# A hybrid SSM, attention and convolution layer on Trainium2: one modulation moved from TensorE to VectorE rows, another shared with GpSimd

## The chip, the cores and the metric

The kernel runs on one core of a Trainium2 chip. The metric is the device time of one execution in microseconds (us), the median over several. A core has TensorE (PE in the profile, with its weight loads as PEld), VectorE (DVE), ScalarE (ACT), GpSimd (POOL) and SyncE (SP), which here issues nearly all DMA transfers. Each engine takes its instructions in a fixed order and waits on semaphores for the others.

## What is computed

One layer of a decoder, 256 tokens, width 2048, float32. It has a token mixer and a gated MLP, each behind an RMSNorm whose scale and shift, and whose gate on the way out, come from a conditioning vector:

```python
cond = jax.nn.silu(c)
mod = cond @ w_mod[l] + b_mod[l]
sh1, sc1, gt1, sh2, sc2, gt2 = jnp.split(mod, 6, axis=-1)
h = rms_norm(x, g_pre_mix[l]) * (1.0 + sc1[:, None]) + sh1[:, None]
y = hybrid_mixer(h, ...)
x = x + gt1[:, None] * rms_norm(y, g_post_mix[l])
h = rms_norm(x, g_pre_ffn[l]) * (1.0 + sc2[:, None]) + sh2[:, None]
y = conv_ffn(h, w_up[l], ffn_conv_w[l], w_down[l])
x = x + gt2[:, None] * rms_norm(y, g_post_ffn[l])
```

The mixer projects `h` to an SSM branch, an attention branch, a convolution branch and three gates of width 2048; `merged` is the sum of the gated branches, and `merged @ w_o` its output. The change concerns `mod`: a vector times a matrix of 2048 x 12288, of which `sc1, sh1` are called half 0, `sc2, sh2` half 1, and `gt1`, `gt2` the two gate modulations.

## The kernel before

**Weights.** All large products are made in fp32r from two parts: a weight tile of 128x1024 is loaded into one of four `raw` buffers, ACT rounds it to `hi` (L72), DVE subtracts to get `lo` (L73, called a split below), and PE makes three products (`mm3`, L123 to L125). `hi` and `lo` have four buffers each; `next_weights` keeps two tiles ahead of the one in use (AHEAD). A stage is therefore a chain of such tiles: four groups of the in-projection (80 tiles), the convolution branch with the attention beside it (24), gate 0, gate 1 and gate 2 (40 each: f = 0 to 15, with two tiles of the gate's projection each and one of the branch's output per two f), the first output projection (32), then the MLP.

**Fillers.** Work that does not belong to the main chain is written as generators that a `Filler` advances at a rate per tick, two ticks per f: the attention, the SSM (beside gates 0 and 1; tables `T`, pairs `M1`, `M2`), the modulations. The language's scheduler then orders each engine's instructions by readiness and priority, so an instruction may stand earlier than it was written.

**Modulation.** Half 1 (`mods2`) has eight groups g of 256 channels. Groups 0 to 3 go by rows on DVE: eight tiles a group, each loaded by `raw_tile` and multiplied with the conditioning row and summed along the row in one instruction (L191), so 32 rows. Groups 4 to 7 (PE_MOD) go on PE (`mod_rows_pe`, `modps`, L152): per four tiles of the sum four matmuls with a 32 column weight, then ACT copies the sums and PE transposes them (`mfps`, L175). Their tiles come alternately through `raw` and one buffer `mraw`. The first gate modulation (`mod_gate`, `gg`) is filled into gate 2 and the output projection: for two halves b of 1024 channels, 16 tiles each (`dx`, five buffers, three loads ahead), DVE accumulates `acc` (L216), then PE sums over the partitions with a matrix of ones (`ggps`, L224).

Of the kernel before, what the change touches and what calls it, by code (L numbers as in the profile page):

```python
# [8 lines left out]
F32 = mybir.dt.float32  # L9
# [6 lines left out]
P = 128  # L16
# [12 lines left out]
LAG = False  # L29
PE_MOD = ((), (4, 5, 6, 7))  # L30

# [18 lines left out]
def kernel(  # L50
# [62 lines left out]

    def next_weights():
        while len(queue) < 1 + AHEAD:
            src = next(stream, None)
            if src is None:
                break
            queue.append(weights(*src))
        return queue.pop(0)  # L120

# [43 lines left out]
    def mod_half(half, g, A_scale, A_shift, vg, vsc, vsh, lag=True):  # L165
        mf = cp.tile([P, 4], F32, tag="mf", name="mf", bufs=2)
        if g in PE_MOD[half]:
            i = PE_MOD[half].index(g)
            res = []
            yield from mod_rows_pe(lambda j: wmod_h[half][i, j], res)  # L170
            if lag:
                yield
            ps = psB.tile([P, 512], F32, tag="B", name="mfps")
            for i in range(4):
                nc.tensor.transpose(  # L175
                    ps[:, P * i : P * i + P], res[0][:, P * i : P * i + P], marks["ident"]
                )
            nc.vector.tensor_reduce(
                mf, ps.rearrange("p (i q r) -> p i q r", i=4, q=4)[:, :, :, 0], AX.X, ALU.add
            )  # L180
        else:
            i = [n for n in range(8) if n not in PE_MOD[half]].index(g)
            mp2 = cp.tile([P, 4, 2], F32, tag="mp2", name="mp2", bufs=2)
            for q in range(4):
                for kc in range(2):
                    if half == 0:
                        w = mp.tile([P, 1024], F32, tag="bo", name="mraw", bufs=6)
                        nc.sync.dma_start(w, wmod_t[half][i, 2 * q + kc])
                    else:
                        w = raw_tile(wmod_t[half][i, 2 * q + kc])  # L190
                    nc.vector.scalar_tensor_tensor(  # L191
                        w, w, 1.0, cond_row[kc], ALU.mult, ALU.mult, accum_out=mp2[:, q, kc : kc + 1]
                    )
                    if q * kc < 3:
                        yield
            nc.vector.tensor_reduce(mf, mp2, AX.X, ALU.add)
# [10 lines left out]

    def mod_gate(which, gg, load, depth):
        for b in range(2):
            acc = sp.tile([P, 1024], F32, tag="acc", name="acc")  # L210
            nc.sync.dma_start(acc, brow[which, b])
            ws = [load(wmod_g[which, b, kt]) for kt in range(depth)]
            for kt in range(KT):
                if kt + depth < KT:
                    ws.append(load(wmod_g[which, b, kt + depth]))
                nc.vector.scalar_tensor_tensor(  # L216
                    acc, ws.pop(0), cond[:, kt : kt + 1], acc, ALU.mult, ALU.add
                )
                yield
            yield  # L220
            for i in range(2):
                c = slice(512 * i, 512 * i + 512)
                ps = psB.tile([P, 512], F32, tag="B", name="ggps")
                nc.tensor.matmul(ps, ones, acc[:, c], start=True, stop=True)  # L224
                nc.vector.tensor_mul(gg[b][:, c], ps, gg[b][:, c])
# [42 lines left out]
    def out_proj(nj, act, gg, ss, yg, tail, filler=None, held=4):  # L268
        for n in range(4):
# [10 lines left out]
            for j in range(cut):  # L280
# [3 lines left out]
                for t in range(2):  # L284
                    mms(j, w, t)
            last = [next_weights() for _ in range(nj - cut)]
            if n == 2:
                dummy = cp.tile([P, 1], F32, tag="dummy", name="dummy")
                nc.scalar.activation(dummy, ss[:, 0, 0:1], AF.Sqrt)
            for t in range(2):  # L290
                for j in range(cut, nj):
                    mms(j, last[j - cut], t)
                with ExitStack() as es:
# [7 lines left out]
                    if n == 3:  # L301
                        tail(t)

    with ExitStack() as mx:
# [330 lines left out]
        def glu(zp):  # L635
# [3 lines left out]
            for f in range(4):  # L639
                ps = psB.tile([P, 512], F32, tag="B", name="glups")  # L640
                for kt in range(4):
                    w = wg[kt // 2]
                    c = 512 * (kt % 2) + P * f
                    mm3(
                        ps[:, :S], w[0][:, c : c + P], w[1][:, c : c + P], gqh[:, kt], gql[:, kt],
                        kt == 0, kt == 3,
# [8 lines left out]
        def ssm_all(zp):  # L655
# [3 lines left out]
            yield  # L659
            gqh = mp.tile([P, 4, S], F32R, tag="bo", name="gqh", bufs=6)  # L660
            gql = mp.tile([P, 4, S], F32R, tag="bo", name="gql", bufs=6)
            ssm_st["g"] = (gq, gqh, gql)
            M1s = [mp.tile([P, 2, S], F32, tag="uv", name="M1", bufs=20) for _ in range(8)]
            M2s = [mp.tile([P, 2, S], F32, tag="uv", name="M2", bufs=20) for _ in range(8)]
            Ts = {}
# [25 lines left out]
            for j in range(4):  # L691
                mm = []
                for q in range(4):
# [12 lines left out]
                    ts_ = T[:, 1].unsqueeze(1).to_broadcast([P, 2, S])  # L706
                    M1, M2 = M1s[s % 8], M2s[s % 8]
                    mm.append((M1, M2))
# [26 lines left out]
                nc.scalar.activation(gq[:, j], yv, AF.Gelu_apprx_tanh)  # L735
                split(gq[:, j], gqh[:, j], gql[:, j])
            glu(zp)
# [47 lines left out]
        fa = fill(attention_all())  # L785
        run(conv_branch(), (fa, 3.5), (m2, 2))
        fa.finish()
# [3 lines left out]
        fs = fill(ssm_all(zp))  # L791
        run(gate_branch(0, 2), (fs, 0.7), (m2, 2))
        run(gate_branch(1, 1), (fs, 0.75), (m2, 1.5))
        fs.finish()
        m2.finish()
        zs.close()
# [10 lines left out]

        mg = fill(mod_gate(0, gg, load_late, 3))
        run(gate_branch(2, 0), (mg, 1.5))
        mg.rate = 1.0  # L810
# [216 lines left out]
```

## Time and profile before

| | us |
|---|---|
| runs, median (lowest, highest) | 1648.1 (1645.53, 1648.68) |
| profiled execution, its own time | 1650.52 |
| its span, first to last instruction | 1648.7 |
| PE busy | 1581.9 |
| DVE busy | 1217.1 |
| ACT busy | 810.2 |
| POOL busy | 61.8 |
| convolution and attention | 284 to 391 |
| gate 0, gate 1, gate 2 | 391 to 536, to 681, to 790 |
| first output projection | 790 to 881 |

The profile shows one execution. Busy time is the union of an engine's instructions; PE's matmuls are pipelined, so the durations of single matmuls overlap. A window gives the busy time of each engine in a stretch of the span; a wait is put down to what released the engine.

### The profile page before, as it was taken

The numbers are of one execution on the slowest core, as the hardware profiler recorded it, in microseconds if no ns is written. First come the engines' busy times: TensorE is split into PE (matmuls) and PEld (weight loads), VectorE is DVE, ScalarE is ACT, GpSimd is POOL, SyncE is SP. The second block draws the span as 40 slices with busy tenths as digits, with TensorE's granted clock in tenths as the row PEclk, the third lists the DMA queues.
The fourth block names the chain that finished last, engine by engine and source line by source line (L and its number), as shares of the span: only waits on it lengthen the run. The fifth ranks groups of instructions, "written<-read, shape, count | busy, mean of one in ns | idle before, by whom it ended". The sixth has DMA issues, their size and how long they took to land.

```text
span 1648.7 us, 26062 instructions
## 1 busy us (share of the span) xinstructions
PE 1581.9 (96%) x10104; PEld 1398.0 (85%) x10104; DVE 1217.1 (74%) x1854; ACT 810.2 (49%) x1219; POOL 61.8 (4%) x102
## 2 busy tenths in 40 slices
PE   2999899999999999999998999999999999999997
PEld 1989889889888899999887888888888888888886
DVE  5889986896787798787757788778888767444444
ACT  2554333655445454544446555555555555344342
POOL 0000940000000000000000000000000000000000
PEclk7999999999999999999999999999999999999999
DMA  8988876777776665888864777767777665666553
GB/s 315 371 322 295 308 263 195 232 248 244 257 258 249 223 225 164 300 315 323 286 190 141 231 240 230 231 217 230 240 233 230 203 192 182 190 190 189 187 188 126
DMA packets 107404, 389.56 MB, mean 236 GB/s; under 512 B 11920, under 2 KB 12048, under 8 KB 107280
## 3 DMA queue, kind: packets, MB, share of 16 engines
q1 hardware_dynamic: 105552, 382.00, 69.1%
q10 hardware_dynamic: 1728, 5.90, 1.0%
q8 instruction: 79, 1.29, 0.3%
q14 instruction: 45, 0.37, 0.1%
HBM read 385.75 MB, written 2.10 MB: 235 GB/s over the span
## 4 chain that ended last, share of the span: by engine, by line
PE 79%; DVE 9%; DMA 6%; ACT 3%; issue 2%; POOL 0%; SPq 0%; DVEq 0%; ACTq 0%
PE ups L876 20%; PE ups L877 10%; PE ops L125 7%; PE ops L124 7%; PE ops L123 7%; PE gps L123 5%; PE gps L125 5%; PE gps L124 5%; PE inps L125 3%; PE inps L124 3%; PE inps L123 3%; DVE lo L73 3%; DMA raw<-in_wmod_t 3%; DMA raw<-in_wB 1%; DVE mraw L191 1%
## 5 line engine op out<-in xcount | busy, mean ns | idle before, releaser
L73 DVE TENSOR_TENSOR lo<-raw,hi 128x1024 fp32r<-128x1024 f32 x520 | 636.1, 1228 | 283.6 <-ACT hi L72 281.8
L72 ACT CAST hi<-raw 128x1024 fp32r<-128x1024 f32 x520 | 541.8, 1047 | 570.1 <-PE ops L125 173.8
L876 PE MATMUL ups<-h2p,hi 128*128 128x512 f32 x1408 | 495.3, 394 | 0.1
L877 PE MATMUL ups<-h2p,lo 128*128 128x256 f32 x1408 | 398.1, 283 | 0.0
L876 PEld LDWEIGHTS ups<-h2p,hi 128*128 128x128 f32 x1408 | 264.4, 188 | 61.7 <-ACT hi L72 0.5
L877 PEld LDWEIGHTS ups<-h2p,lo 128*128 128x128 f32 x1408 | 264.7, 188 | 0.6 <-issue 0.5
L123 PE MATMUL gps<-hh,hi 128*128 128x256 f32 x768 | 219.3, 286 | 0.0
L125 PE MATMUL gps<-hh,lo 128*128 128x256 f32 x768 | 216.5, 282 | 2.1 <-DVE lo L73 2.1
L124 PE MATMUL gps<-hl,hi 128*128 128x256 f32 x768 | 216.4, 282 | 0.0
L123 PEld LDWEIGHTS gps<-hh,hi 128*128 128x128 f32 x768 | 144.9, 189 | 15.3 <-issue 8.0
L123 PE MATMUL inps<-hh,hi 128*128 128x256 f32 x448 | 128.2, 287 | 23.6 <-ACT hi L72 23.6
L125 PEld LDWEIGHTS gps<-hh,lo 128*128 128x128 f32 x768 | 144.7, 188 | 2.3 <-DVE lo L73 2.3
L124 PEld LDWEIGHTS gps<-hl,hi 128*128 128x128 f32 x768 | 144.8, 189 | 0.2 <-issue 0.2
L123 PE MATMUL ops<-hi,ah 128*128 128x512 f32 x352 | 138.9, 395 | 0.0
L124 PE MATMUL ops<-lo,ah 128*128 128x512 f32 x352 | 138.9, 395 | 0.0
L125 PE MATMUL ops<-hi,al 128*128 128x512 f32 x352 | 138.9, 395 | 0.0
L125 PE MATMUL inps<-hh,lo 128*128 128x256 f32 x448 | 128.3, 289 | 4.4 <-DVE lo L73 4.4
L124 PE MATMUL inps<-hl,hi 128*128 128x256 f32 x448 | 127.6, 286 | 0.0
L123 PEld LDWEIGHTS inps<-hh,hi 128*128 128x128 f32 x448 | 86.4, 193 | 24.4 <-ACT hi L72 24.2
L125 PEld LDWEIGHTS inps<-hh,lo 128*128 128x128 f32 x448 | 85.8, 192 | 6.0 <-DVE lo L73 6.0
L191 DVE SCALAR_TENSOR_TENSOR mraw<-mraw,cond_row 128x1024 f32<-128x1024 f32 x64 | 78.4, 1236 | 16.1 <-DMA mraw<-in_wmod_t 16.1
L124 PEld LDWEIGHTS inps<-hl,hi 128*128 128x128 f32 x448 | 86.2, 193 | 0.1
(244 smaller groups left out, 2324.1 us busy)
## 6 DMA issues: line engine op xcount, KB each, us to landing
raw<-in_wup SPq DMA_DIRECT2D x176, 512.0 KB, 4.2
raw<-in_wB SPq DMA_DIRECT2D x120, 512.0 KB, 4.5
raw<-in_wdn SPq DMA_DIRECT2D x88, 512.0 KB, 3.6
raw<-in_wA SPq DMA_DIRECT2D x80, 512.0 KB, 5.1
mraw<-in_wmod_t SPq DMA_DIRECT2D x64, 512.0 KB, 5.5
raw<-in_wmod_t SPq DMA_DIRECT2D x32, 512.0 KB, 4.5
dx<-in_wmod_g SPq DMA_DIRECT2D x32, 512.0 KB, 6.5
raw<-in_wo SPq DMA_DIRECT2D x32, 512.0 KB, 4.0
```

The lines of the kernel that those rows point to most:

```text
L72: marks["act"] = nc.scalar.copy(hi, src)
L73: nc.vector.tensor_sub(lo, src, hi)
L123: nc.tensor.matmul(dst, wh, ah, start=first, stop=False)
L124: nc.tensor.matmul(dst, wh, al, start=False, stop=False)
L125: nc.tensor.matmul(dst, wl, ah, start=False, stop=last)
L191: nc.vector.scalar_tensor_tensor(w, w, 1.0, cond_row[kc], ALU.mult, ALU.mult, accum_out=mp2[:, q, kc : kc + 1])
L876: nc.tensor.matmul(ps, wh[:, c], hp, start=kt == 0, stop=False)
L877: nc.tensor.matmul(ps[:, 0], wl[:, c], hp[:, 0], start=False, stop=kt == KT - 1)
```

## The change

All eight groups of half 1 go as DVE rows (PE_MOD is empty for both halves), 64 rows instead of 32. Their tiles no longer use `raw_tile` but one buffer `mraw`, whose load is issued one step ahead of its row. The filler's rates are 1.4, 1.2, 1.2 and 1.4 instead of 2, 2 and 1.5, and it now runs on into gate 2. In the first gate modulation every tile with an odd number goes to GpSimd, which scales it by the condition and adds it to two tiles `accp` of 512 columns; a second matmul per half of 512 columns adds `accp` to `ggps`. The SSM gets six pairs M1 and M2 instead of eight, and `gqh`, `gql` lie in other buffers. `out_proj` looks ahead less at the end of its last tiles and fetches one tile after each half of the tokens instead.

```diff
-PE_MOD = ((), (4, 5, 6, 7))
+PE_MOD = ((), ())
...
-    def next_weights():
-        while len(queue) < 1 + AHEAD:
+    def prefetch(n):
+        while len(queue) < n:
...
+    def next_weights(ahead=AHEAD):
+        prefetch(1 + ahead)
         return queue.pop(0)
...
+            def load(n):
+                tag, bufs = ("bo", 6) if half == 0 else ("mraw", 1)
+                w = mp.tile([P, 1024], F32, tag=tag, name="mraw", bufs=bufs)
+                nc.sync.dma_start(w, wmod_t[half][i, n])
+                return w
+
             for q in range(4):
                 for kc in range(2):
-                    if half == 0:
-                        w = mp.tile([P, 1024], F32, tag="bo", name="mraw", bufs=6)
-                        nc.sync.dma_start(w, wmod_t[half][i, 2 * q + kc])
-                    else:
-                        w = raw_tile(wmod_t[half][i, 2 * q + kc])
+                    w = load(2 * q + kc)
+                    if half == 1:
+                        yield
                     nc.vector.scalar_tensor_tensor(
                         w, w, 1.0, cond_row[kc], ALU.mult, ALU.mult, accum_out=mp2[:, q, kc : kc + 1]
                     )
...
-    def mod_gate(which, gg, load, depth):
+    def mod_gate(which, gg, load, depth, split_with=None):
...
+                w = ws.pop(0)
+                if split_with is not None and kt % 2:
+                    for i in range(2):
+                        c = slice(512 * i, 512 * i + 512)
+                        k = cond[:, kt : kt + 1]
+                        if kt == 1:
+                            part.append(split_with())
+                            nc.gpsimd.tensor_scalar(part[i], w[:, c], k, None, ALU.mult)
+                        else:
+                            nc.gpsimd.tensor_scalar(w[:, c], w[:, c], k, None, ALU.mult)
+                            nc.gpsimd.tensor_add(part[i], part[i], w[:, c])
+                else:
+                    nc.vector.scalar_tensor_tensor(
+                        acc, w, cond[:, kt : kt + 1], acc, ALU.mult, ALU.add
+                    )
                 yield
...
-                nc.tensor.matmul(ps, ones, acc[:, c], start=True, stop=True)
+                nc.tensor.matmul(ps, ones, acc[:, c], start=True, stop=not part)
+                if part:
+                    nc.tensor.matmul(ps, ones, part[i], start=False, stop=True)
...
-            last = [next_weights() for _ in range(nj - cut)]
+            last = [next_weights(min(AHEAD, nj - 1 - j)) for j in range(cut, nj)]
...
+                prefetch(t + 1)
...
-            M1s = [mp.tile([P, 2, S], F32, tag="uv", name="M1", bufs=20) for _ in range(8)]
+            M1s = [mp.tile([P, 2, S], F32, tag="uv", name="M1", bufs=20) for _ in range(6)]
...
-        run(conv_branch(), (fa, 3.5), (m2, 2))
+        run(conv_branch(), (fa, 3.5), (m2, 1.4))
...
-        run(gate_branch(0, 2), (fs, 0.7), (m2, 2))
-        run(gate_branch(1, 1), (fs, 0.75), (m2, 1.5))
+        run(gate_branch(0, 2), (fs, 0.7), (m2, 1.2))
+        run(gate_branch(1, 1), (fs, 0.75), (m2, 1.2))
...
-        run(gate_branch(2, 0), (mg, 1.5))
+        run(gate_branch(2, 0), (mg, 1.5), (m2, 1.4))
+        m2.finish()
```

The order of the instructions shows the change at three places. The first is SP's queue of transfers at the start of gate 0 (`raw<-in_wB`, `in_wbr`: weight tiles; `in_wmod_t`: tiles of the half-1 rows; `in_wmod_h`: tiles of the PE path; x2 is two in a row). Before:

```order
L66 DMA raw<-in_wbr 128x1024
L66 DMA raw<-in_wB 128x1024
L66 DMA raw<-in_wmod_t 128x1024
L66 DMA raw<-in_wB 128x1024
L66 DMA raw<-in_wmod_t 128x1024
L66 DMA raw<-in_wB 128x1024 x2
L66 DMA raw<-in_wmod_t 128x1024 x2
L66 DMA raw<-in_wbr 128x1024
```

After, at the same place:

```order
L66 DMA raw<-in_wbr 128x1024
L191 DMA mraw<-in_wmod_t 128x1024
L66 DMA raw<-in_wB 128x1024 x2
L191 DMA mraw<-in_wmod_t 128x1024
L66 DMA raw<-in_wB 128x1024
L191 DMA mraw<-in_wmod_t 128x1024
L66 DMA raw<-in_wB 128x1024
L66 DMA raw<-in_wbr 128x1024
```

The modulation's tiles have left the `raw` buffers, and each has its turn behind the row that frees `mraw`.

The second place is DVE in the middle of gate 0 (`lo<-raw,hi`: a split; `T`, `M`: the SSM; `mrg`: the gated sum). Before, where no row is left:

```order
L677 SCALAR_TENSOR_TENSOR T<-T,PC,tt 128x128
L681 SCALAR_TENSOR_TENSOR T<-T,PC,tt 128x128
L73 TENSOR_TENSOR lo<-raw,hi 128x1024
L761 TENSOR_TENSOR mrg<-gps,sg 128x256
L73 TENSOR_TENSOR lo<-raw,hi 128x1024 x3
L761 TENSOR_TENSOR mrg<-gps,sg 128x256
L709 TENSOR_TENSOR M_4463<-px,T 128x512
```

After:

```order
L705 SCALAR_TENSOR_TENSOR T<-T,PC,tt 128x128
L709 SCALAR_TENSOR_TENSOR T<-T,PC,tt 128x128
L199 SCALAR_TENSOR_TENSOR mraw,mp_5909<-mraw,cond_row 128x1024
L73 TENSOR_TENSOR lo<-raw,hi 128x1024 x2
L789 TENSOR_TENSOR mrg<-gps,sg 128x256
L199 SCALAR_TENSOR_TENSOR mraw,mp_5909<-mraw,cond_row 128x1024
L73 TENSOR_TENSOR lo<-raw,hi 128x1024
L199 SCALAR_TENSOR_TENSOR mraw,mp_5909<-mraw,cond_row 128x1024
L73 TENSOR_TENSOR lo<-raw,hi 128x1024 x2
L789 TENSOR_TENSOR mrg<-gps,sg 128x256
L737 TENSOR_TENSOR M_4422<-px,T 128x512
```

Three modulation rows stand between the splits, with one to three other instructions from one to the next.

The third place is PE in gate 2, where the first half of the gate modulation is summed over the partitions. Before:

```order
L124 MATMUL gps<-bol,hi 128x256
L125 MATMUL gps<-boh,lo 128x256
L224 MATMUL ggps<-acc,ones 128x512 x2
L123 MATMUL gps<-hh,hi 128x256
L124 MATMUL gps<-hl,hi 128x256
```

After:

```order
L127 MATMUL gps<-bol,hi 128x256
L128 MATMUL gps<-boh,lo 128x256
L247 MATMUL ggps<-acc,ones 128x512
L249 MATMUL ggps<-accp,ones 128x512
L247 MATMUL ggps<-acc,ones 128x512
L249 MATMUL ggps<-accp,ones 128x512
L126 MATMUL gps<-hh,hi 128x256
```

Two matmuls more, which wait for GpSimd's sums, stand in PE's row.

## Rows read from the trace of the kernel before

**Rows 1.** Page, part 1: busy us (share of the span) and number of instructions.

```profile
PE 1581.9 (96%) x10104; PEld 1398.0 (85%) x10104; DVE 1217.1 (74%) x1854; ACT 810.2 (49%) x1219; POOL 61.8 (4%) x102
```

**Rows 2.** Windows by stage: length; busy of PE, PEld, DVE, ACT, POOL; clock; DMA.

```profile
230.00:284.00 54.00, 54.00 (x386) 50.82 (x385) 33.81 (x39) 18.94 (x19) 0.00 (x0) 1.00 0.65 221
284.00:391.00 107.00, 101.76 (x842) 91.55 (x841) 91.53 (x189) 64.49 (x121) 0.00 (x0) 1.00 0.73 243
391.00:536.00 145.00, 138.90 (x1140) 124.59 (x1140) 108.50 (x219) 68.90 (x117) 0.00 (x0) 0.99 0.71 251
536.00:681.00 145.00, 144.73 (x1249) 134.82 (x1249) 120.43 (x226) 76.24 (x119) 0.00 (x0) 1.00 0.65 209
681.00:789.80 108.80, 106.74 (x887) 105.57 (x886) 91.00 (x110) 49.86 (x66) 0.00 (x0) 1.00 0.91 331
```

**Rows 3.** PE: groups (busy us, mean ns, idle before); windows of `modps`, then `mfps`.

```profile
L152 PE MATMUL modps<-mraw,condp 128*32 128x512 f32 x64 | 16.8, 605 | 2.7 <-DMA mraw<-in_wmod_h 2.5
...
391.00:536.00 145.00, 11.72 (x88) 0.99 0.71 251
536.00:681.00 145.00, 5.33 (x40) 1.00 0.65 209
...
sum 397.00, PE 2.51; mean PE 0.84
```

**Rows 4.** PE's waits: who waited for whom, us in total, times, longest.

```profile
PE modps L152 <- DMA mraw<-in_wmod_h: 2.5, 4, 1.1
```

**Rows 5.** Groups by line and shape, DVE and PE: busy us, mean ns, idle before.

```profile
L73 DVE TENSOR_TENSOR lo<-raw,hi 128x1024 fp32r<-128x1024 f32 x520 | 636.1, 1228 | 283.6 <-ACT hi L72 281.8 <-PE modps L152 1.3
L191 DVE SCALAR_TENSOR_TENSOR mraw<-mraw,cond_row 128x1024 f32<-128x1024 f32 x64 | 78.4, 1236 | 16.1 <-DMA mraw<-in_wmod_t 16.1
L216 DVE SCALAR_TENSOR_TENSOR acc<-dx,cond,acc 128x1024 f32<-128x1024 f32 x32 | 40.9, 1279 | 1.6 <-DMA acc<-in_brow 1.4
L191 DVE DVE_READ_ACCUMULATOR mraw<-mraw,cond_row 128x1 f32 x64 | 5.2, 81 | 0.0
...
L224 PE MATMUL ggps<-acc,ones 128*128 128x512 f32 x16 | 7.5, 592 | 0.0
```

**Rows 6.** Loads of `mraw` from 432 to 600 us; SP and DVE timelines, gate 0.

```profile
DMA to landing us min/median/max: 4.3/4.7/6.8
...
398.22 1.94 SPq L66 DMA_DIRECT2D raw<-in_wmod_t  x2
406.48 0.33 SPq L66 DMA_DIRECT2D raw<-in_wmod_t  x1
...
402.74 1.23 DVE L191 SCALAR_TENSOR_TENSOR raw<-raw,cond_row 128x1024 f32<-128x1024 f32 x1 [1.76 <-DMA raw<-in_wmod_t]
412.61 1.23 DVE L191 SCALAR_TENSOR_TENSOR raw<-raw,cond_row 128x1024 f32<-128x1024 f32 x1 [2.54 <-DMA raw<-in_wmod_t]
```

**Rows 7.** DVE's waits, gate 0 and then gate 1: us in total, times, longest.

```profile
DVE lo L73 <- ACT hi L72: 23.2, 17, 3.7
DVE T L677 <- ACT tt L674: 3.1, 7, 0.6
...
DVE sg L652 <- ACT sg L649: 2.3, 1, 2.3
```

**Rows 8.** Timelines of POOL and DVE, 172 to 191 us: start, duration, count.

```profile
175.52 1.05 POOL L409 TENSOR_TENSOR CQ<-CT,fr 128x512 f32<-128x512 f32 x1
181.78 2.47 POOL L415 TENSOR_SCALAR CQ<-CQ 128x512 f32<-128x512 f32 x1
188.20 2.28 POOL L416 TENSOR_TENSOR CQ<-CQ,tq 128x512 f32<-128x512 f32 x1
...
172.46 2.37 DVE L73 TENSOR_TENSOR lo<-raw,hi 128x1024 fp32r<-128x1024 f32 x2
180.58 3.85 DVE L73 TENSOR_TENSOR lo<-raw,hi 128x1024 fp32r<-128x1024 f32 x2
188.09 3.46 DVE L73 TENSOR_TENSOR lo<-raw,hi 128x1024 fp32r<-128x1024 f32 x2
```

More of the change, by code (lines that the diff above doesn't have):

```diff
@@ L193, in mod_half @@
                     )
-                    if q * kc < 3:
+                    if half == 0 and q * kc < 3:
                         yield
@@ L212, in mod_gate @@
             ws = [load(wmod_g[which, b, kt]) for kt in range(depth)]
+            part = []
             for kt in range(KT):
@@ L215, in mod_gate @@
                     ws.append(load(wmod_g[which, b, kt + depth]))
-                nc.vector.scalar_tensor_tensor(
-                    acc, ws.pop(0), cond[:, kt : kt + 1], acc, ALU.mult, ALU.add
-                )
+                w = ws.pop(0)
[13 more added lines that the diff above has]
+                    )
                 yield
             yield
+            if part:
+                yield
             for i in range(2):
@@ L223, in mod_gate @@
                 ps = psB.tile([P, 512], F32, tag="B", name="ggps")
-                nc.tensor.matmul(ps, ones, acc[:, c], start=True, stop=True)
+                nc.tensor.matmul(ps, ones, acc[:, c], start=True, stop=not part)
+                if part:
+                    nc.tensor.matmul(ps, ones, part[i], start=False, stop=True)
                 nc.vector.tensor_mul(gg[b][:, c], ps, gg[b][:, c])
@@ L644, in glu @@
                     mm3(
-                        ps[:, :S], w[0][:, c : c + P], w[1][:, c : c + P], gqh[:, kt], gql[:, kt],
+                        ps[:, :S], w[0][:, c : c + P], w[1][:, c : c + P], gqh[kt // 2][:, kt % 2], gql[kt // 2][:, kt % 2],
                         kt == 0, kt == 3,
@@ L659, in ssm_all @@
             yield
-            gqh = mp.tile([P, 4, S], F32R, tag="bo", name="gqh", bufs=6)
-            gql = mp.tile([P, 4, S], F32R, tag="bo", name="gql", bufs=6)
+            gqh, gql = (
+                [mp.tile([P, 2, S], F32R, tag="uv", name="gqx", bufs=20) for _ in range(2)]
+                for _ in range(2)
+            )
             ssm_st["g"] = (gq, gqh, gql)
-            M1s = [mp.tile([P, 2, S], F32, tag="uv", name="M1", bufs=20) for _ in range(8)]
-            M2s = [mp.tile([P, 2, S], F32, tag="uv", name="M2", bufs=20) for _ in range(8)]
+            M1s = [mp.tile([P, 2, S], F32, tag="uv", name="M1", bufs=20) for _ in range(6)]
+            M2s = [mp.tile([P, 2, S], F32, tag="uv", name="M2", bufs=20) for _ in range(6)]
             Ts = {}
@@ L706, in ssm_all @@
                     ts_ = T[:, 1].unsqueeze(1).to_broadcast([P, 2, S])
-                    M1, M2 = M1s[s % 8], M2s[s % 8]
+                    M1, M2 = M1s[s % 6], M2s[s % 6]
                     mm.append((M1, M2))
@@ L735, in ssm_all @@
                 nc.scalar.activation(gq[:, j], yv, AF.Gelu_apprx_tanh)
-                split(gq[:, j], gqh[:, j], gql[:, j])
+                split(gq[:, j], gqh[j // 2][:, j % 2], gql[j // 2][:, j % 2])
             glu(zp)
@@ L791 @@
         fs = fill(ssm_all(zp))
-        run(gate_branch(0, 2), (fs, 0.7), (m2, 2))
-        run(gate_branch(1, 1), (fs, 0.75), (m2, 1.5))
+        run(gate_branch(0, 2), (fs, 0.7), (m2, 1.2))
+        run(gate_branch(1, 1), (fs, 0.75), (m2, 1.2))
         fs.finish()
-        m2.finish()
         zs.close()
@@ L806, in load_late @@
             return w
-        mg = fill(mod_gate(0, gg, load_late, 3))
-        run(gate_branch(2, 0), (mg, 1.5))
+        mg = fill(mod_gate(
+            0, gg, load_late, 3, lambda: mp.tile([P, 512], F32, tag="uv", name="accp", bufs=20)
+        ))
+        run(gate_branch(2, 0), (mg, 1.5), (m2, 1.4))
+        m2.finish()
         mg.rate = 1.0
```

## The prediction, made before the result was known

> **What bounds the kernel now.** I read the page's busy shares first, then the windows cut at the stages, then who waits for whom inside a stage. TensorE (PE) is busy 96% of the span [rows 1]. The windows show where the rest lies. The change touches the last in-projection group, the convolution, gates 0 to 2 [rows 2] and the first output projection behind them. There PE is full or nearly full in every stage, so an instruction taken off PE shortens the span, as long as VectorE (DVE) keeps up. DVE is the next engine: 91.5 of 107 us in the convolution, 108.5 and 120.4 of 145 in gates 0 and 1, 91.0 of 108.8 in gate 2. That is the number to watch: the change takes work from PE and gives more to DVE, where little room is left.
>
> **What leaves PE.** The four groups of half 1 that PE computes are 128 matmul instructions. Each of their two forms shows 16.8 us busy, but the forms run side by side (32 columns each), and both together have 11.7 us in gate 0 and 5.3 in gate 1; the transposes of the sums have 2.5, about half in either [rows 3]. PE also waited 2.5 us there for loads [rows 4]. So PE gives back 17.0 + 2.5 + 2.5 = 22 us at most, some 15 of it in gate 0 and 7 in gate 1. The ACT copies and small reduces that go with it are beside PE.
>
> **What DVE gets.** 32 more rows, each 1.236 us and 0.08 for the read of its accumulator [rows 5], 1.3 together: 42 us. Where they land I counted in the order against the splits of the weight tiles, since rates of the fillers do not tell (the scheduler hoists them): 8 of the 64 rows stand in the last in-projection group, 16 in the convolution, 20 in gate 0, 14 in gate 1, 6 in gate 2. Before, all 32 stand in convolution and gate 0. So convolution to gate 1 (397 us) has 50 rows instead of 32: 18 x 1.3 = 23 us on top of 91.5 + 108.5 + 120.4 = 320.4, or 343. PE there needs 101.8 + 138.9 + 144.7 = 385.4 less 19.6 of work, 366; with the convolution's idle 5 us, which come from attention, and the waits gone, some 375. DVE would have to be 92% busy just to let PE have its gain. It has been there for short stretches only.
>
> **The single buffer.** Before, a row's tile came through the four `raw` buffers; now all half-1 tiles share one `mraw`. The load of row n+1 waits on SP for row n to leave DVE, and DVE then waits for the load. What such a load takes, issue to landing, is shown by the `mraw` loads of the PE path in the same gates: 4.3 at least, median 4.7 us; and by two loads for DVE: issued 398.22, its row started 402.74 (4.5 us), issued 406.48, started 412.61 (6.1, behind two others) [rows 6]. Between two rows the order leaves DVE other work. Adding the durations of that work, less 0.06 us each, since neighbours overlap (a split has 1.228 [rows 5], two in a row 2.37 [rows 8]), 36 of the 50 rows have less than 4.7 us in front of them, mostly 2.5 to 3.7 (one split of 1.2 and a few short ones); the fence on DVE shows pairs with one to three splits between. The missing time sums to 40 us for loads of 4.2 us, 57 for 4.7. Some of it is not lost: where the order leaves hardly anything between two rows, DVE would have waited for PE's buffers. I take off about 10 and use 38 of the range 20 to 57. SP itself loses nothing by the wait, since each such load stands behind four `raw` loads already issued, as deep as the buffers go.
>
> DVE in this stretch is then 343 + 38 + 9 (waits of the kind now in gates 0 and 1, of which the longest two of seven are 3.1 and 2.3 [rows 7]) = 390 us against 397 now. The gain is 7 us, where PE alone would allow 22. Bounds: 375 (loads hidden, PE bounds, -22) and 409 (all of 57 lost, +12).
>
> **The last in-projection group.** 8 rows more: 33.8 + 10.4 + about 8 of missing time, 52 us of 54 [rows 2]. It just fits; 0 to 3, I take 1.
>
> **Gate 2.** Five of its six rows fall within the first ten weight tiles. DVE has 34 us there with 5 us of missing load time, before 25.5; ten tiles of PE are 108.8/4 = 27. So about 6 us of lag, of which the two tiles split ahead may cover some: 0 to 8, I take 5. PE gets more work: the sum over partitions now needs a second matmul per half. 16 instructions in 8 halves are busy 7.5 us [rows 5], 0.94 a half; two halves more in gate 2, two in the output projection, 1.9 us each.
>
> **GpSimd.** It takes 16 of the 32 tiles: 60 instructions of 128x512. DVE saves 16 x 1.28 = 20.5 us. What the GpSimd instructions cost is seen around 175 to 191 us, where eight of that size ran: 1.05 us while DVE was idle or reading PSUM, 2.47 beside DVE's splits, 14.96 for all eight with one short one between, so 1.87 each at most; two splits took 2.37 us just before and 3.85 and 3.46 during it [rows 8]. The four splits lost 2.6 us, the modulation rows among them some 0.9 by my estimate from the share of the splits: 0.43 per GpSimd instruction. So 60 cost DVE 26 us: the offload gives DVE nothing. With some 40 of them in gate 2, DVE there is 91.0 - 14 x 1.28 + 6 x 1.3 + 40 x 0.43 = 98 of 108.8, and PE still bounds after the start. GpSimd's own pace: 30 instructions per half of the sum at 1.87 us are 56 us, and the order leaves 24 weight tiles (65 us) for the first half and 22 (61) for the second before PE meets the matmul that waits for GpSimd. SP waits for GpSimd too: a tile's buffer comes free only when its sum is done, and `raw` loads stand behind that wait. At 1.87 both fit, at 2.47 (74 us) they lack 9 and 13. I take 1 per half, 0 to 10 each. DMA in gate 2 is at 331 GB/s with share 0.91; only 6 more tiles come into it, but also a reason why loads there are rather late than early.
>
> **Rest.** The changed look-ahead at the end of the output projection moves nothing that counts: from its last weight tiles on, the rows of DVE and ACT read alike in both orders. Six M pairs instead of eight are free: a pair comes round six steps later, long after its readers. All at nothing.
>
> **Sum** against the profiled run, 1650.5 us (span 1648.7 and 1.8 around it): -7 + 1 + (1.9 + 5 + 1) + (1.9 + 1) = +5, 1655. The runs' median, 1648.1, is 2.4 lower, so 1653.
>
> **Rivals.**
> *DVE keeps up (faster).* The missing load time falls where DVE has to wait for PE's buffers anyway: in gate 0 it now waits 23.2 us for ACT's copies, which wait for buffers [rows 7]. For it: this slack. Against it: with PE quicker the slack goes. Stretch 376 (-21), gate 2 and projection +6, in-projection +1: -14, or 1634. It wins if the missing time in the stretch stays under about 25 us.
> *GpSimd and DVE shut each other out (much slower).* The eight instructions did not block DVE for their whole 1.05 us [rows 8], but splits there alternated with PSUM reads; in gate 2 nearly all of DVE's work reads two SBUF tensors. If each of 40 takes 1.05 from DVE, DVE has 91 - 18 + 8 + 42 = 123 us of 108.8, +14 +1.9; 30 instructions of 2.47 in the output projection are 74 us for 61, +13 +1.9. With -6 before: +25, 1673. The point from which it decides is some 0.7 us per GpSimd instruction.
> The Trainium skill, page "SBUF — State Buffer", section "Who interferes with whom", states that rule: a DVE instruction with two SBUF inputs and a GpSimd instruction that reads SBUF exclude each other for the whole instruction. The trace agrees that both stretch, but shows 0.43 us per instruction, not the whole; by the rule the sum would be this rival's.
> *The gain pays just for the additions.* The PE matmuls come back as stalls of equal size and the sum is zero: 1648.
>
> **How the numbers follow.** My forecast case (DVE bounds, 1642 to 1662, likeliest 1653) has 0.50, DVE keeps up (1628 to 1642) 0.24, the lock-out (1662 to 1685) 0.16, zero (1645 to 1651) 0.10. The range is 1634 to 1673: it cuts about 0.09 off each end. A measurement here tells 0.2%, 3.3 us: faster below 1644.8 is 0.24 and 0.04 of the forecast case; same 0.10 and 0.11 of it; slower the rest, 0.51.
>
> **What would show it.** Right: `modps` gone, DVE's row in gates 0 and 1 at 90% or more, DVE waiting 25 to 50 us for `mraw` loads, PE waiting in these gates for DVE's splits, which it hardly does now; conv to gate 1 between 385 and 397 us; splits in gate 2 stretched by some 0.3 us each. Wrong: DVE's waits on `mraw` under 20 us with PE still full (then the faster rival), or PE waiting for GpSimd at the summing matmul by over 5 us (then the slower).

## The result, and the profile after

The changed kernel takes 1661.4 us (median of 4 runs, 1656.6 to 1662.5) against 1647.8 for the kernel before: ratio 1.0083, 95% interval [1.0066, 1.0099], so 13.6 us slower. A second set of six runs gave 1.0089 [1.0071, 1.0107]. The profiled execution took 1661.99, its span is 1660.2 (before 1648.7).

Page of the changed kernel, part 1, as [rows 1]:

```profile
PE 1572.8 (95%) x9968; PEld 1396.3 (84%) x9968; DVE 1260.2 (76%) x1902; ACT 808.1 (49%) x1215; POOL 177.9 (11%) x162
```

PE is busy 9 us less and the span is 11.5 longer: PE waits more. To see where, I cut both executions at the same places of the program: 284 (start of the convolution), the first matmul of gate 0, the last of gate 1, the first of the output projection, the first of the MLP. The fixed cuts of [rows 2] end gate 0 some 4 us and gate 1 some 17 us later than these matmuls do, so the kernel before stands here too, first. Columns: length; busy time (and number) of PE, PEld, DVE, ACT, POOL; clock; DMA share, GB/s.

```profile
284.00:391.20 107.20, 101.96 (x844) 91.75 (x843) 91.73 (x189) 64.49 (x121) 0.00 (x0) 1.00 0.73 244
391.20:531.70 140.50, 134.40 (x1106) 121.44 (x1104) 104.48 (x214) 67.06 (x115) 0.00 (x0) 0.99 0.72 252
531.70:663.80 132.10, 131.83 (x1123) 121.63 (x1121) 112.56 (x212) 65.72 (x103) 0.00 (x0) 1.00 0.64 204
663.80:789.90 126.10, 124.04 (x1047) 121.81 (x1046) 102.79 (x128) 62.22 (x85) 0.00 (x0) 1.00 0.88 320
789.90:896.30 106.40, 100.80 (x455) 81.61 (x453) 69.97 (x104) 54.74 (x95) 0.00 (x0) 0.98 0.60 199
```

The changed kernel:

```profile
284.00:389.50 105.50, 100.82 (x841) 91.05 (x840) 84.55 (x172) 64.61 (x120) 0.00 (x0) 1.00 0.68 218
389.50:523.30 133.80, 123.08 (x1017) 117.82 (x1016) 112.66 (x224) 64.76 (x110) 0.00 (x0) 1.00 0.66 222
523.30:656.80 133.50, 126.49 (x1067) 120.21 (x1065) 126.85 (x245) 65.86 (x103) 0.00 (x0) 1.00 0.65 212
656.80:792.60 135.80, 128.66 (x1051) 123.69 (x1050) 114.02 (x130) 59.33 (x82) 83.38 (x43) 1.00 0.83 301
792.60:907.50 114.90, 104.53 (x459) 83.53 (x457) 77.97 (x105) 57.00 (x98) 34.45 (x18) 0.97 0.62 210
```

Convolution to gate 1 went from 379.8 to 372.8 us, a gain of 7.0. Gate 2 lost 9.7 and the output projection 8.5 (e1 and e2 below divide gate 2's 9.7 into 6.2 for the rows and 3.5 for GpSimd's share). The MLP behind them is unchanged (752.4 us to the end of the span before, 752.7 after). The first half of the change pays, and its end gives back more.

**The gain.** DVE's waits and PE's waits of the changed kernel, 284 to 656.8 us (us in total, times, longest):

```profile
DVE mraw L199 <- DMA mraw<-in_wmod_t: 37.4, 27, 3.5
...
PE gps L128 <- DVE lo L73: 17.3, 17, 2.6
```

DVE is busy 84.55 + 112.66 + 126.85 = 324.1 of these 372.8 us. It stands 37.4 before rows whose tile is not there, and 11.4 for other things; that is the whole length, within 0.1. DVE sets the pace here, and PE, which waited once for a split before, waits 17 times.

**The loss in the projection.** SP, POOL, DVE and PE of the changed kernel, 786 to 805 us (start, duration, engine, line, [idle before it and what ended that]):

```profile
791.13 0.33 SPq L66 DMA_DIRECT2D raw<-in_wo  x1
795.26 0.80 SPq L832 DMA_DIRECT2D dx<-in_wmod_g  x2
...
803.40 2.60 SPq L66 DMA_DIRECT2D raw<-in_wo  x2
...
786.59 5.87 POOL L234 TENSOR_SCALAR dx<-dx,cond 128x512 f32<-128x512 f32 x2
792.43 2.81 POOL L235 TENSOR_TENSOR accp<-accp,dx 128x512 f32<-128x512 f32 x2
...
799.89 1.28 DVE L237 SCALAR_TENSOR_TENSOR acc<-dx,cond,acc 128x1024 f32<-128x1024 f32 x1 [3.15 <-DMA dx<-in_wmod_g]
801.09 2.28 DVE L73 TENSOR_TENSOR lo<-raw,hi 128x1024 fp32r<-128x1024 f32 x1
...
803.43 0.50 PE L127 MATMUL ops<-lo,mh 128*128 128x512 f32 x1 [3.59 <-DVE lo L73]
```

Read it backwards. PE stood 3.59 us for a split that ended at 803.4. The split stood behind an accumulation that waited 3.15 us for its `dx` tile. That tile had been asked for only at 795.26, since its buffer was held by GpSimd until 792.43 + 2.81 = 795.24. GpSimd had needed 5.87 us for two scalings and 2.81 for two additions, 8.7 us for one tile. So PE here waits for GpSimd through a buffer, SP's queue, a load and DVE, and no wait of PE or DVE names GpSimd. SP's own waits do (656.8 to 907.5 us):

```profile
SPq L832 <- POOL accp L235: 22.5, 6, 7.3
```

Not all of the 3.59 us is the buffer's: the last split took 2.28 us beside GpSimd, where one alone takes 1.23. The next view, windows around it, shows what it cost beyond the idle time:

```profile
798.00:803.00 5.00, 1.84 (x8) 1.15 (x7) 3.11 (x2) 1.05 (x1) 5.00 (x4) 1.00 0.97 391
803.00:808.00 5.00, 4.57 (x13) 3.65 (x14) 5.00 (x7) 1.61 (x3) 5.00 (x3) 0.66 0.61 155
```

After the idle 3.6 us the granted clock in the next window is 0.66: eight matmuls ran at the lower level (1.2 GHz), 0.43 us apart instead of 0.23, which is 1.5 us more. Idle 0.75 + 3.59, the clock's 1.5 and the extra matmuls (1.4, measured below) make 7.2 of the 8.5; the rest isn't accounted for.

**GpSimd and DVE beside each other.** Groups of the changed kernel, 656.8 to 907.5 us (busy us, mean ns | idle before). For comparison, [rows 5] has 1279 ns for the accumulation and 1228 for a split; the last three lines are the kernel before, 663.8 to 896.3 us:

```profile
L73 DVE TENSOR_TENSOR lo<-raw,hi 128x1024 fp32r<-128x1024 f32 x76 | 107.2, 1422 | 32.1 <-ACT hi L72 31.7 <-issue 0.3
...
L73 DVE TENSOR_TENSOR ml<-mrg,mh 128x256 fp32r<-128x256 f32 x16 | 13.1, 818 | 0.9 <-ACT mh L72 0.9
L792 DVE TENSOR_TENSOR mrg<-mrg,sg 128x256 f32<-128x256 f32 x17 | 11.2, 661 | 0.3
...
L234 POOL TENSOR_SCALAR dx<-dx,cond 128x512 f32<-128x512 f32 x28 | 64.6, 2317 | 24.0 <-DVE mrg L792 17.3 <-DMA dx<-in_wmod_g 4.4 <-DVE lo L73 2.2
L235 POOL TENSOR_TENSOR accp<-accp,dx 128x512 f32<-128x512 f32 x28 | 46.2, 1669 | 0.0
L237 DVE SCALAR_TENSOR_TENSOR acc<-dx,cond,acc 128x1024 f32<-128x1024 f32 x16 | 25.0, 1561 | 7.4 <-DMA acc<-in_brow 4.2 <-DMA dx<-in_wmod_g 3.2
...
L73 DVE TENSOR_TENSOR lo<-raw,hi 128x1024 fp32r<-128x1024 f32 x74 | 90.2, 1222 | 42.9 <-ACT hi L72 42.7
L764 DVE TENSOR_TENSOR mrg<-mrg,sg 128x256 f32<-128x256 f32 x17 | 7.1, 420 | 0.2
L73 DVE TENSOR_TENSOR ml<-mrg,mh 128x256 fp32r<-128x256 f32 x16 | 6.7, 418 | 0.9 <-ACT mh L72 0.9
```

Count times the longer mean, these four kinds of DVE instruction take some 30 us more in the changed kernel (15 for the `lo` splits, 6 for `ml`, 4 for `mrg`, 4.5 for the accumulations). DVE is spared 16 accumulations, 20.5 us. So the offload adds to DVE's work.

### The profile page after: what moved, and what is told of

Read it like the earlier page. It is cut to its first block, busy times and chain, and to the rows that moved or that the text cites. A ratio compares the mean times of both kernels' runs of the same rounds, so it can differ in the third digit from the quotient of the medians.

```text
span 1660.2 us, 25898 instructions
## 1 busy us (share of the span) xinstructions
PE 1572.8 (95%) x9968; PEld 1396.3 (84%) x9968; DVE 1260.2 (76%) x1902; ACT 808.1 (49%) x1215; POOL 177.9 (11%) x162
## 3 DMA queue, kind: packets, MB, share of 16 engines
q8 instruction: 78, 1.28, 0.3%
## 4 chain that ended last, share of the span: by engine, by line
PE 61%; DVE 19%; DMA 12%; issue 5%; ACT 2%; POOL 0%; SPq 0%; DVEq 0%; ACTq 0%
PE ups L906 20%; PE ups L907 10%; DMA mraw<-in_wmod_t 10%; PE ops L127 7%; PE ops L128 7%; PE ops L126 7%; DVE lo L73 6%; DVE mraw L199 4%; PE gps L128 2%; PE gps L126 2%; PE gps L127 2%; PE inps L128 2%; PE inps L127 2%; PE inps L126 1%; DVE M L743 1%
## 5 line engine op out<-in xcount | busy, mean ns | idle before, releaser
L73 DVE TENSOR_TENSOR lo<-raw,hi 128x1024 fp32r<-128x1024 f32 x520 | 647.7, 1252 | 233.8 <-ACT hi L72 232.8
L199 DVE SCALAR_TENSOR_TENSOR mraw<-mraw,cond_row 128x1024 f32<-128x1024 f32 x128 | 158.1, 1241 | 71.0 <-DMA mraw<-in_wmod_t 70.7
```

The lines of the kernel that those rows point to most:

```text
L73: nc.vector.tensor_sub(lo, src, hi)
L199: nc.vector.scalar_tensor_tensor(w, w, 1.0, cond_row[kc], ALU.mult, ALU.mult, accum_out=mp2[:, q, kc : kc + 1])
```

## The experiments

Theory A at the start was that GpSimd's share costs more than it saves, and that the single buffer of the rows costs the rest. Each run is timed against the kernel before on the same chip. The windows below are cut as above, at gate 2 and the projection.

**e1: the rows without GpSimd.** In the changed kernel:

```diff
-        mg = fill(mod_gate(
-            0, gg, load_late, 3, lambda: mp.tile([P, 512], F32, tag="uv", name="accp", bufs=20)
-        ))
+        mg = fill(mod_gate(0, gg, load_late, 3))
```

> The changed kernel, but the whole gate modulation stays on DVE (no GpSimd share, no second summing matmul); the 64 rows and their single buffer stay. Theory A, GpSimd costs more than it saves: in the changed kernel the last 14 f of gate 2 lose about 5 us against the kernel before and the first output projection 8.5, of which the extra summing matmuls are 1.9 each; without the share the projection goes from its first matmul to the first one of the MLP in 106.5 to 108 us instead of 115, gate 2 gets 2 to 4 us shorter, DVE's splits there are back at 1.23 us, and the kernel takes about 1649 us (1646 to 1652). Rival B, the share relieves a DVE that the rows fill: DVE has 20 us more of its own work in gate 2 and the projection, PE waits there for splits, and the kernel takes 1661 us or more.

Measured: 1648.2 us, ratio 0.9998 [0.9987, 1.0009]. Gate 2 and projection:

```profile
655.00:787.30 132.30, 127.09 (x1048) 124.05 (x1047) 109.07 (x145) 62.51 (x85) 0.00 (x0) 0.99 0.89 325
787.30:893.10 105.80, 100.14 (x455) 81.61 (x453) 70.81 (x105) 54.67 (x94) 0.00 (x0) 0.98 0.63 207
```

The projection is back, gate 2 is 3.5 us shorter than in the changed kernel and still 6.2 longer than before. The 64 rows (with the smaller edits that came with them) come out at zero by the medians; in the profiled execution they gain 9 us up to the end of gate 1 (ends at 655.0, before 663.8) and lose 6 in gate 2. Rival B falls.

**e2: GpSimd's share alone.** The kernel before with the changed `mod_gate`, rows and PE groups as they were.

> The kernel before, with the GpSimd share of the first gate modulation as the only change (32 rows and the PE groups as before). Theory A, the share costs by itself: 3.8 us of matmuls and 5 to 8 us of stretched splits and of loads that wait on SP for GpSimd, in gate 2 and at the start of the projection: 1657 us (1654 to 1660), the projection 113 to 115 us long. Rival B, the share only hurts beside the rows that run late into gate 2: nothing but the matmuls, 1650 to 1652 us.

Measured: 1661.3 us, ratio 1.0080 [1.0065, 1.0094]. That is 1.3 us over theory A's range and 9 over rival B's.

```profile
662.20:791.80 129.60, 126.41 (x1051) 122.74 (x1051) 106.36 (x111) 59.00 (x82) 85.38 (x42) 1.00 0.79 287
791.80:907.60 115.80, 105.51 (x458) 84.38 (x456) 77.13 (x105) 57.14 (x97) 35.41 (x19) 0.96 0.63 210
```

The share costs 12.6 us by itself, without any row there; by the windows 3.5 in gate 2 and 9.4 in the projection. With e1 this adds up: 0.9998 and 1.0080 against 1.0083 and 1.0089 for both.

**e3: row loads from GpSimd's queue.** In the changed kernel:

```diff
-                nc.sync.dma_start(w, wmod_t[half][i, n])
+                (nc.sync if half == 0 else nc.gpsimd).dma_start(w, wmod_t[half][i, n])
```

> The changed kernel, with the loads of the half 1 rows issued from GpSimd's queue instead of SP's; buffer and rows as in the changed kernel. Theory A, SP's queue is part of the loss: a load of a row waits on SP until the row before has left DVE (136.9 us of such waits), and weight tiles whose buffers are free stand behind it, as at 666 to 672.6 us at the end of gate 1; on another queue the weight tiles come up to some us earlier and the 8 us that are lost from f = 29 of gate 1 to the start of gate 2 go: 1653 us (1650 to 1656). Rival C, what costs is DVE itself, which stands 70.7 us before rows whose load is not there, whoever issues it: 1660 to 1663 us with the same waits.

Measured: 1680.4 us, ratio 1.0193 [1.0180, 1.0206]. Convolution to gate 1 took 374.6 us (changed kernel 372.8; gate 0 4.8 shorter, gate 1 4.2 longer), so with SP free of these waits no gain shows, and DVE's waits for the rows' loads stayed (39.3 us there, 37.4 in the changed kernel): SP's queue was not what cost there. The total is 17 us over rival C's range too. In gate 2 (152.1 us long) the loads stand in GpSimd's row behind its sums; waits there:

```profile
POOL mraw L191 <- DVE mraw L199: 24.6, 5, 7.8
DVE mraw L199 <- DMA mraw<-in_wmod_t: 14.0, 5, 5.7
PE gps L128 <- DVE lo L73: 12.9, 4, 6.4
```

GpSimd waits for a row of DVE before it can issue the next load and go on with its sums, and DVE waits for that load. The part of theory A about SP falls.

**e4: the rows through `raw`.** In the changed kernel:

```diff
+                if half == 1:
+                    return raw_tile(wmod_t[half][i, n])
```

> The changed kernel, with the tiles of the half 1 rows loaded through the four raw buffers, as in the kernel before, instead of the single buffer. Theory A, the single buffer is what costs in convolution to gate 1: DVE's waits for row loads fall from 70.7 us to under 25, gates 0 and 1 end 5 to 10 us earlier, and the kernel takes 1653 us (1650 to 1657), with the loss by GpSimd left. Rival D, the rows take the places of weight tiles in the raw buffers, ACT's and DVE's splits come later and PE waits for them: as slow as the changed kernel or slower, 1660 to 1668 us.

Measured: 1673.4 us, ratio 1.0143 [1.0127, 1.0158]. DVE's waits for row loads fell to 24.3 us between 284 and 680, and gate 1 ended at 651.8, 5 us earlier. But the order shifted with the buffers: 16 rows instead of 6 ran in gate 2, which got 17.5 us longer:

```profile
651.80:805.10 153.30, 136.87 (x1051) 129.59 (x1050) 124.68 (x160) 61.92 (x85) 74.59 (x38) 0.96 0.84 302
```

From convolution to gate 1 DVE was busy 320.0 of 367.8 us, in the changed kernel 324.1 of 372.8: it stood as long as before. What it no longer waited for rows it waited for ACT's copies (18.6 us instead of 7.8), and ACT for weight tiles of `in_wB` (45.4 instead of 10.2), as rival D had it. The earlier end goes with less work there (two rows of the ten were moved out of this stretch, eight out of the in-projection group before it). So it is not shown that the single buffer costs time in the gates, as A said. The total (expected 1653) was missed by 20 us, with ten rows more where DVE has least room; neither theory had that, and as a test of the buffer by itself the run is spoiled.

**e5: every fourth tile.** As e2, with

```diff
-                if split_with is not None and kt % 2:
+                if split_with is not None and kt % 4 == 1:
```

> The kernel before with the GpSimd share as its only change, as in e2_pool_only (1661.3 us against 1648.7), but GpSimd takes every fourth tile instead of every second: 8 tiles and 28 instructions instead of 16 and 60; the extra summing matmuls are all there. Theory A, pace: a tile takes GpSimd some 8.4 us, the projection gives it 5.6 us per second tile, so it holds the dx buffers, SP waits for them with the weight tiles behind it, and PE stops; with every fourth tile it has time, and only the matmuls (3.4 us by their busy time) are left: 1652 us (1651 to 1654). Theory B, stretch: each GpSimd instruction costs DVE, and so PE, a share; half of the 9 us beyond the matmuls is left: 1656 to 1658 us.

Measured: 1654.7 us, ratio 1.0042 [1.0027, 1.0056], 7 us over the kernel before. This lies between the two: beyond the matmuls some 4 us are left of 9.5. SP still waits 7.6 us for GpSimd once, and the projection is 110.7 long. The run doesn't separate the theories.

**e6: the loaded tile is set free earlier.** As e2, with the product in tiles of its own:

```diff
-                            nc.gpsimd.tensor_scalar(w[:, c], w[:, c], k, None, ALU.mult)
-                            nc.gpsimd.tensor_add(part[i], part[i], w[:, c])
+                            nc.gpsimd.tensor_scalar(scr[i], w[:, c], k, None, ALU.mult)
+                            nc.gpsimd.tensor_add(part[i], part[i], scr[i])
```

> As e2_pool_only (1661.3 us), but GpSimd writes its product to two tiles of its own instead of back into the loaded tile, so that the dx buffer is free after the two scalings (about 4.7 us) and not after the two additions (about 8.4); all instructions and their number as there. Theory A, pace and the held buffer: SP's waits for GpSimd fall from some 26 us to about 10, DVE's waits for dx loads at the start of the projection go, 1655 to 1658 us. Theory B, stretch: the same instructions cost the same, 1660 to 1663 us.

Measured: 1654.8 us, ratio 1.0037 [1.0021, 1.0053]. The same number of instructions, as slow as before, cost some 6 us less (5.5 by the medians, 7 by the ratios):

```profile
662.80:792.10 129.30, 127.01 (x1052) 123.41 (x1051) 105.35 (x113) 60.98 (x85) 85.45 (x43) 1.00 0.83 301
792.10:899.90 107.80, 102.11 (x459) 82.56 (x457) 77.94 (x103) 54.85 (x96) 35.29 (x18) 0.98 0.63 210
```

SP's waits for GpSimd (676 to 830 us) fell from 15.0 to 1.2 us, the projection from 115.8 to 107.8, and PE has no idle time at its start. The held buffer is what costs in the projection beyond the matmuls, whose run, e8 below, has the same 107.8.

**e7: GpSimd beside DVE, nothing shared.** The kernel before, DVE does all its tiles, and behind every odd one GpSimd has

```diff
+                        if kt == 1:
+                            nc.gpsimd.tensor_scalar(part[i], gg[b][:, c], k, None, ALU.mult)
+                        else:
+                            nc.gpsimd.tensor_scalar(part[2 + i], part[i], k, None, ALU.mult)
+                            nc.gpsimd.tensor_add(part[i], part[i], part[2 + i])
```

> The kernel before, with 60 GpSimd instructions of 128x512 added in the gate modulation that work on tiles of their own and that nobody waits for; DVE still does all 32 tiles, PE has no matmul more. It measures the stretch alone. Theory A, pace: DVE's splits in gate 2 are stretched to about 1.4 to 1.6 us on average, DVE has room for most of it, PE loses 0 to 4 us: 1649 to 1653 us. Theory B, stretch: the 9 us beyond the matmuls come from here, and since DVE does all its tiles too, the loss is 9 us or more: 1658 to 1668 us.

Measured: 1666.5 us, ratio 1.0117 [1.0098, 1.0137]. Gate 2 by the window:

```profile
665.90:809.00 143.10, 128.09 (x1047) 124.09 (x1046) 133.20 (x124) 58.55 (x83) 118.69 (x60) 0.98 0.77 271
```

Groups of DVE between 676 and 860 us:

```profile
L73 DVE TENSOR_TENSOR lo<-raw,hi 128x1024 fp32r<-128x1024 f32 x58 | 86.7, 1508 | 12.4 <-ACT hi L72 12.2
L216 DVE SCALAR_TENSOR_TENSOR acc<-dx,cond,acc 128x1024 f32<-128x1024 f32 x32 | 49.6, 1549 | 2.3 <-DMA acc<-in_brow 1.4 <-DMA dx<-in_wmod_g 0.8
```

DVE is busy 1251.4 us in all against 1217.1 [rows 1]: 34.3 us for 60 instructions, 0.57 each, and gate 2 is 17 us longer. Theory B is right that the stretch is real, and A was wrong to give it 0 to 4. All 60 instructions fell into gate 2 here, since nobody waits for them; the changed kernel, with some 40 there and the rest in the projection, had 30 us of stretch, as counted above.

**e8: the matmuls alone.** The kernel before with a second summing matmul on a tile of zeros:

```diff
-                nc.tensor.matmul(ps, ones, acc[:, c], start=True, stop=True)
+                nc.tensor.matmul(ps, ones, acc[:, c], start=True, stop=zero is None)
+                if zero is not None:
+                    nc.tensor.matmul(ps, ones, zero, start=False, stop=True)
```

> The kernel before, with the second summing matmul of each half of 512 columns as the only change (its operand is a tile of zeros, GpSimd does no tile). It prices the matmuls alone: by the busy time of the 16 matmuls of the changed kernel against the 8 of the kernel before, 7.2 against 3.8 us, 3.4 us, all on a full PE: 1651.1 us against 1647.7 (1650 to 1652.5). If other work hides them: 1647 to 1649.

Measured: 1651.5 us, ratio 1.0019 [1.0005, 1.0033], by the ratio 3.1 us (by the medians 2.2). Gate 2 is 127.5 us long (before 126.1), the projection 107.8 (106.4): 1.4 each.

So of the 12.6 us of the share some 3 are matmuls and 5.5 to 7 the held buffers (e2 less e6, by the medians and by the ratios). Some 3 are left. They would be what DVE loses by the stretch beyond what it is spared, but this part comes by subtraction: no run shows it alone.

**e9 and e10: e6's edit in the changed kernel, and the changed kernel again.**

> The changed kernel, with GpSimd's products in two tiles of its own, as in e6_dx_early, so that a loaded tile is free after the two scalings. If the held dx buffers cost in the changed kernel what they cost beside 32 rows (12.6 us fell to 7.1 or 6.3 by the ratios), it takes 1655 us (1653 to 1657) instead of 1661.4, nearly all of the gain in the output projection, which then takes 107 to 109 us instead of 115. If the rows in gate 2 decide instead: 1659 to 1662.

> The changed kernel once more, unchanged, for a narrower interval than its first [1.0066, 1.0099] and for a second profile, since e9_change_dx_early (1.0066 of before, [1.0045, 1.0086]) overlaps it. If the held dx buffers cost in the changed kernel too, it stands at 1.0075 to 1.010 and its projection again takes about 115 us against 109 in e9; if e9's edit brings nothing here, it stands at 1.0066 as well. The second profile also shows by how much gates 0 and 1 differ from one execution of the same program to another (5.5 us between the changed kernel and e9, whose programs are the same up to gate 2).

Measured: e9 1658.9 us, 1.0066 [1.0045, 1.0086]; e10 1662.1, 1.0089 [1.0071, 1.0107]. The projection of e9 by its window:

```profile
798.80:907.70 108.90, 102.14 (x458) 82.31 (x456) 79.18 (x104) 56.17 (x96) 36.63 (x18) 0.98 0.65 213
```

That of e10:

```profile
792.00:907.60 115.60, 105.30 (x459) 84.78 (x457) 76.17 (x104) 57.20 (x98) 34.00 (x18) 0.96 0.62 209
```

The projection is 6 to 7 us shorter, as expected. The total isn't settled: it moved by some 4 us, with intervals that overlap, and 1658.9 lies above the 1653 to 1657 that were expected. The profiled execution of e9 is one of the longer of its set (1662.4). In it the convolution began at 285.9 and gate 1 ended at 662.3, in those of the changed kernel at 283.8 and 282.0, and at 656.8 and 655.5, before any edited instruction ran; why is open. The runs that share the kernel before's order of instructions up to gate 2 (e2, e5 to e8) ended gate 1 between 661.7 and 665.9, so a single such figure is good to a few us.

**g1 and g2: rows behind the crowded place.** The rows without GpSimd, the last 16 (g1) or 24 (g2) of them in the projection, through the `dx` buffers, three loads ahead; g1:

```diff
-        run(gate_branch(1, 1), (fs, 0.75), (m2, 1.2))
+        run(gate_branch(1, 1), (fs, 0.75), (m2, 0.8))
...
-        run(gate_branch(2, 0), (mg, 1.5), (m2, 1.4))
-        m2.finish()
+        run(gate_branch(2, 0), (mg, 1.5), (m2, 0.3))
...
+            late = half == 1 and g >= LATE
+            ws = [marks["load_late"](wmod_t[half][i, n]) for n in range(3)] if late else []
```

> A version without the GpSimd share (as e1_no_pool, 1648.2 us), in which 48 of the 64 rows stay in convolution to gate 2 at lower rates in gates 1 and 2 and the last 16 go into the output projection, loaded through the five dx buffers three ahead. In e1_no_pool gates 0 and 1 were 10 us ahead of the kernel before at f = 31 and lost 5 to 7 of it around the start of gate 2, where rows, the SSM's last steps and the gate modulation meet on DVE. Theory E, that meeting is what eats the gain of the PE groups: moved behind it, some 5 to 8 us stay: 1640 to 1644 us, the projection not over 108 us long. Rival F, the gain is not to be kept, DVE pays for the rows wherever they stand (the projection has 27 us of 87 free, 16 rows are 21): 1646 to 1652 us with a longer projection.

> As g1_rows_late (1640.7 us), but 24 rows instead of 16 in the output projection, and none of the others written into gate 2. If rows in gate 1 still cost PE something: 1637 to 1640 us. If the projection's DVE (60 of 87 us busy without rows, 24 rows are 31 us) or the dx buffers, shared with the gate modulation there, become the limit: 1642 to 1648, the projection over 108 us long.

Measured: g1 1640.7 us, 0.9952 [0.9936, 0.9969]; g2 1641.0, 0.9953 [0.9936, 0.9970]. Gate 1, gate 2 and projection of g1:

```profile
523.80:652.60 128.80, 126.12 (x1067) 121.14 (x1065) 117.28 (x223) 65.89 (x103) 0.00 (x0) 0.99 0.58 181
652.60:780.60 128.00, 125.94 (x1048) 123.72 (x1047) 102.99 (x128) 62.29 (x85) 0.00 (x0) 0.99 0.88 314
780.60:886.50 105.90, 100.37 (x455) 81.85 (x453) 88.58 (x144) 54.67 (x94) 0.00 (x0) 0.98 0.77 280
```

The projection of g2:

```profile
771.60:884.60 113.00, 102.28 (x454) 81.25 (x452) 98.33 (x164) 55.07 (x94) 0.00 (x0) 0.97 0.80 301
```

In g1 gate 1 is 4.7 us shorter than in the changed kernel, gate 2 loses 1.9 instead of 6.2, and the projection hides its 16 rows in DVE's free time. It beats both kernels by 7 and 21 us. These 16 rows also changed their loading (`dx` buffers, three ahead, instead of one buffer), so the run doesn't show how much of the 7 us comes from the place and how much from the buffers. In g2 gate 2 starts 7 us earlier still, and the projection, 7 longer, takes it back; its total lies between its two forecasts.

## Why the prediction was right, and where its size was off

The direction was right, and 1661 lies in the range; the size, +5 against the profiled run, was less than half of what came. That much is weak: the range is 39 us wide and holds both signs, slower had a chance of 0.51, and 1661.4 lies at the edge between the forecast case and the lock-out. By its steps:

- **What leaves PE.** PE's busy time from convolution to gate 1 fell from 368.2 to 350.4 us, 17.8, near the 17.0 + 2.5 of the sum; the two or three of waits went too, and 17.3 of new waits came.
- **Rows and single buffer.** The gain of 7 came out as 7.0, and that it meets so closely is luck. The missing load time was 37.4 us (38 taken), other waits 11.4 (9): the mechanism, DVE pacing the stretch by its work and its waits for loads, is borne out. But by the same rule these cuts give 308.8 + 23 = 332 for DVE's own work and, with 38 and 9, 379 of 379.8 us, a gain of 1; the work was 324. The few us by which such ends differ between executions (e9) are in the 7.0 as well. That the wait costs nothing on SP is borne out by e3, which took it off SP without a gain in this stretch. DVE is busy 84% of gate 0 and 95% of gate 1, where 90 was named as the sign; `modps` is gone.
- **The last in-projection group.** Taken at 1: the first convolution matmul ran at 283.8 instead of 284.5, and at 282.0 in the second profile, so nothing shows.
- **Gate 2.** Lag of 5 for the rows: 6.2 in e1. The working behind it is off, though. It took 27 us for ten weight tiles from a window that opens 17 us after gate 2's first matmul; by the 126.1 us of its 40 tiles they are 31.5, and the same sum gives 2.5. The rows by the sum were -7 + 1 + 5 = -1; e1 measured 0 within 0.1%.
- **GpSimd: the term that was mis-sized.** The share was to cost 1.9 + 1 in each of gate 2 and projection, 5.8 in all; e2 measured 12.6. The matmuls were 1.4 each. The step that failed reads: "30 instructions per half of the sum at 1.87 us are 56 us, and the order leaves 24 weight tiles (65 us)", and "At 1.87 both fit". The pace was nearly right (2317, 1669 and 1936 ns, 1.99 in the mean), and PE never waited at the summing matmul. But a half as a whole is the wrong measure: each tile holds one of five buffers for some 8 us (8.7 for the one above), while the projection, with 2.8 us for a weight tile and one gate tile with each, asks for one of GpSimd's every 5.6. SP stops at the next load, with DVE's tile and the weight tiles behind it, and PE stops long before the half's end. The prediction named this queue and gave it 0 to 10 per half; the projection took 8.0 of that (115.8 in e2 against 107.8 in e6 and e8), where 1 was taken.
- **The stretch.** 0.43 per GpSimd instruction was taken; e7 measured 0.57, and the changed kernel's 30 us make 0.50. "The offload gives DVE nothing" holds with a worse sign. The splits in gate 2 and the projection were longer by 0.20 us in the mean (1422 against 1222 ns); for gate 2 some 0.3 was named as the sign.
- **The rivals.** DVE did not keep up. The lock-out rival gave 0.7 as its point, and 0.57 is near it, but its way wasn't the main one: e6 leaves the stretch in and takes away about half of the share's loss. The zero rival's 1648 is what e1 measured, without GpSimd's share; the whole change missed it by 13 us.
- **Rest.** At nothing: e1's projection is 0.6 shorter than before, the MLP the same.

## What to carry to other kernels

When an engine takes over part of a stream whose tiles come through shared buffers and one queue, compare the time it holds a buffer with the time between two such tiles, tile by tile: a total that fits hides a queue that stops. Write its result elsewhere, so that the buffer is free after one read. And work that may run late belongs where the engine really is free: the same 64 rows gained nothing when they ended in gate 2, and 7 us when their last 16 ran in the projection, loaded three ahead.

## What the runs showed of the hardware

- DVE's instructions beside GpSimd are stretched in steps, not evenly. While GpSimd worked in e7, an `ml` split of 128x256 took 0.41 us (8 of 13) or up to 1.52, an accumulation 1.28 to 2.32 (half of the 20 at 1.6 to 1.7), a `lo` split 1.21 (11 of 33) or up to 2.33. The longest are 1.0 to 1.1 us more, about what a GpSimd instruction of 128x512 took alone (1.05 in [rows 8]). The products `sg<-gps,sg`, which read one operand from PSUM, kept 0.41 to 0.43, all 13. So DVE's instructions with two operands in SBUF are the ones that are stretched; that such a step is the wait for one whole GpSimd instruction fits its size, but no run shows it instruction by instruction. The Trainium skill (page "SBUF — State Buffer", section "Who interferes with whom") states that a DVE instruction with two SBUF inputs contends with a GpSimd instruction that reads SBUF. The trace agrees; the mean of 0.57 over all 60 is measured here and not given there.
- An idle stretch of PE can cost more than its length: behind the 3.6 us in the changed kernel's projection the granted clock was 0.66 over 5 us, with eight matmuls at the lower level, 1.5 us on top.
- Loads issued from GpSimd's queue stand behind its arithmetic and make that arithmetic wait for them (24.6 us of waits in gate 2 of e3): e3 lost 19 us against the changed kernel, 16 of them in gate 2.
